# Branch B's query and key projections as four Strassen pairs in a stage of their own

## Chip, core and metric

One core of a Trainium2 chip runs the whole layer in one launch. The metric is device time in microseconds (us), the median of the runs. Of the core's engines, TensorE (PE, with PEld for its weight loads) does matmuls and transposes, VectorE (DVE), ScalarE (ACT) and GpSimd (POOL) work on tiles, and SyncE (SP) issues most DMAs.

## What is computed

An encoder layer is applied to two sequences, of 512 and of 1024 tokens, with 1024 features each; what concerns this change:

```
xn = RMSNorm(x);  z = xn @ W_in -> q_A k_A v_A q_B k_B v_B gate_A gate_B
branch A: grouped-query attention (8 query heads, 2 key heads, 64 wide, q/k normed, rotary)
branch B: 8 heads of neighbourhood attention: a key window of 8 rows x 16 columns on a
          grid 64 wide, learned relative bias; q_B, k_B are 512 columns each
mix = (sigmoid(gate_A) * (o_A @ W_pA) + sigmoid(gate_B) * (o_B @ W_pB)) @ W_out
x = x + mix;  x = x + relu(RMSNorm(x) @ W_up)^2 @ W_down;  final RMSNorm
```

All is float32. A matmul operand is split into a high part that the fp32r format holds and a remainder; `mm3` forms one product from three matmuls: high by high, high by low, low by high.

## The kernel before

`run` works through one sequence: the short one first (`NB == 1` block of 512 tokens), then the long one (`NB == 2`). The MLP follows for both. Within `run`, for each of the two key heads `g` of branch A, stage `phR` projects q, k, v (and v of branch B) and stage `phA` does the attention in units of one head and 512 queries, eight per `g` in the long sequence. Then stage `phB` does branch B, and `phG` the merge and `W_out`.

The gates need 128 x 8 x 3 large matmuls in all for the long sequence. They are generators (`gate`) put into `fill`: each `fill.pull(n)` traces n steps of them, a step being three matmuls of 128x128 by 128x512, so that TensorE has work while the softmax of the stage runs. In `phA`, each unit has eight key chunks (`kc`); in each, four transposes of P, the split of P by ScalarE and VectorE, two matmuls into o, and one pull in six of the eight chunks. What is left is drained at the end of the stage. In `phB`, a unit is a head and a strip of 16 columns (32 units); in each, `s_unit` (scores, bias, softmax), `t_unit` of the unit before (transposes) and `v_unit` of the one before that, with five or six pulls between.

Queries and keys of branch B are projected in `phB` by `qkproj`, one pair of heads at a time: for the first pair at the stage's start, for each of the next three within units 6 and 7 of the eight that precede it. A projection of 128 columns takes 8 feature slices x `mm3` for each of two token blocks, for q and for k: 96 matmuls a pair, 384 in all. From PSUM the result goes by ScalarE (high) and VectorE (low) straight to the tiles `qB` and `kB`. Each head's high and low parts lie in the two halves of the 128 partitions, so that one matmul sums over both.

The 8 KB-per-partition tiles (xn, q, k, v strips, gate weights) are slots of two pools: `s8r` with 11 slots on the right, `s8l` with 6 on the left. A new tile waits until a slot is free.

The order on each engine is made by a planner: it takes instructions whose inputs and buffers it expects to be ready, the earlier traced first. `tc.keep_in_program_order` pins an instruction behind the one traced before it on its engine.

The MLP's up projection (`up`) is already a Strassen scheme of seven products on 128x128 by 128x384 matmuls. Its operands are made by `up_steps` and, for the activations, by `pair_t`, in which some sums lie on GpSimd.

Of the kernel before, what the change touches and what calls it, by code (L numbers as in the profile page):

```python
# [61 lines left out]
def encoder(ctx: ExitStack, tc: tile.TileContext, xs, outs, w):  # L62
# [316 lines left out]
    def run(tr, nxt, first):  # L379
# [89 lines left out]
        def load_v(g, alloc, pin=False):  # L469
            return load_cols(win, 1792 + 256 * g, 256, f"v{N}_{g}", alloc, pin)  # L470

        early = {}
        for g in range(2):
            with phase(f"phR{N}_{g}") as ph:
                xn_of = {}
                fresh = g == 0 and tr.ready < NT
# [190 lines left out]
            with phase(f"phA{N}_{g}") as ph:  # L667
                units = [(h, qb) for h in range(4) for qb in range(NB)]
                PP = {}

                def s_tile(u, j):
                    h, qb = u
                    nm = f"{N}_{g}_{h}_{qb}_{j}"
                    q0 = (qb * 4 + j) * P
                    lhs = qT[h % 2][:, h // 2, q0 : q0 + P]
                    s = big(f"s{nm}")[:, :T]
                    for kb in range(NB):
                        ks = slice(kb * 512, kb * 512 + 512)
# [24 lines left out]

                for j in range(4):
                    s_tile(units[0], j)
                    fill.pull(2)
                queue = []
                LAG = 2
                for ui, u in enumerate(units):
                    h, qb = u  # L710
                    if first:
                        bias_row(g * 4 + ui)
                        if g == 0 and ui == 1:
                            early["a"] = load_a(1)
                        if g == 0 and ui == 2:
                            early["v"] = load_v(1, slot)
                    nxt_u = units[ui + 1] if ui + 1 < len(units) else None
                    sdone = 0
                    for kc in range(NT):
                        pt = mm(f"pT{N}_{g}_{h}_{qb}_{kc}")  # L720
                        for j in range(4):
                            nc.tensor.transpose(  # L722
                                pt[:, j * P : (j + 1) * P], PP[u, j][:, kc * P : (kc + 1) * P], ident
                            )
                        hi = ph.tile([P, 512], F32R, tag="pth", name=f"pth{N}_{g}_{h}_{qb}_{kc}", bufs=3)
                        lo = ph.tile([P, 512], F32R, tag="ptl", name=f"ptl{N}_{g}_{h}_{qb}_{kc}", bufs=3)
                        nc.scalar.activation(hi, pt, AF.Copy)  # L727
                        nc.vector.tensor_tensor(lo, pt, hi.bitcast(F32), op=ALU.subtract)  # L728
                        queue.append((u, kc, hi, lo))
                        if nxt_u is not None:  # L730
                            while sdone < 4 and kc >= ((0, 1, 3, 4) if NB == 2 else (0, 0, 1, 2))[sdone]:
                                s_tile(nxt_u, sdone)
                                sdone += 1

                        fill.pull(1 if NB == 1 or kc % 4 < 3 else 0)
                        if len(queue) > LAG:
                            pv(*queue.pop(0))
                fill.drain()
                for item in queue:
                    pv(*item)  # L740

        mA = {}
        wp_b = []
# [44 lines left out]
        with phase(f"phB{N}") as ph:  # L788
# [4 lines left out]
            def prep(h):  # L793
                rc = ph.tile([P, 16, 48], F32, tag="rect", name=f"rect{N}_{h}", bufs=2)
                nc.sync.dma_start(rc, biases[:, :, h].rearrange("r c i j -> (r c) i j"))
                rects[h] = rc
                v = slot([P, 4, rows // 4, P], F32R, f"vs{N}_{h}")
                for j in range(4):
                    c0 = (0, 8, 24, 32)[j]
                    for a in range(4):  # L800
                        nc.sync.dma_start(
                            v[a * 32 : a * 32 + 32, j, :, :].bitcast(F32),
                            vd[:, h, :].rearrange("(k a c) d -> a c k d", a=4, c=GRID_W)[a, c0 : c0 + 32],
                        )
                strips[h] = v

            def load_qk(pr):
                return (
                    load_cols(win, 768 + pr * P, P, f"bq{N}_{pr}"),
                    load_cols(win, 1280 + pr * P, P, f"bk{N}_{pr}"),  # L810
                )

            def qkproj(pr, wqk, dest):
# [4 lines left out]
                for tb in range(NB):  # L818
# [31 lines left out]
                    for e in range(2):  # L850
# [4 lines left out]
                        for os_ in (hs, ls):  # L855
                            nc.vector.tensor_tensor(
                                kT[e][os_, 1, cs], pk[hs], kT[e][hs, 0, cs].bitcast(F32), op=ALU.subtract
                            )

            qk = {}  # L860
            def s_unit(u):
                h, j = u
# [84 lines left out]
                    hi, lo = (oX3[0][ps, i, j * nq : (j + 1) * nq] for i in range(2))  # L947
                    finish_o(o, nq, None, ph, f"B{nm}", (hi, lo, ps))

            prep(0)  # L950
            fill.add(gate(3328, zg[1]))
            wqk = load_qk(0)
            fill.pull(1)
            for _ in qkproj(0, wqk, qk):
                pass
            units = [(h, j) for h in range(8) for j in (1, 2, 0, 3)]
            n = len(units)
            LS, LV = (1, 1) if NB == 2 else (2, 1)
# [1 line left out]
            for i in range(n + LS + LV):  # L960
                if i < n - 8:
                    f = (5 if i < LS else 2 + i % 2) if NB == 1 else 5 + (i % 3 > 0)
                else:
                    f = 3 + i % 2 if NB == 1 else 7
                if i < n:
                    s_unit(units[i])
                    if units[i][1] == 1 and units[i][0] + 1 < 8:
                        prep(units[i][0] + 1)
                    if i % 8 == 6 and i + 2 < n:

                        qp = qkproj(i // 8 + 1, wqk, qk)
                        for _ in range(NC8):
                            next(qp)
                    if i % 8 == 7 and qp is not None:
                        for _ in qp:
                            pass
                        qp = None
                        if i + 1 < n - 8:
                            wqk = load_qk(i // 8 + 2)
                fill.pull(f // 2)  # L980
                if 0 <= i - LS < n:
                    t_unit(units[i - LS])
                if i == n - (12 if first else 8):
                    pa = proj_a(ph)
                    next(pa)
                if i == n - 8:
                    fill.drain()
                    fill.add(pa)
                if i == 3:
                    wqk = load_qk(1)  # L990
                if qp is not None and NB == 2:
                    for _ in range(NC8):
                        next(qp)
                fill.pull(f - f // 2)
                if 0 <= i - LS - LV < n:
                    v_unit(units[i - LS - LV])
# [710 lines left out]
```

## Time and profile before

| | us |
|---|---|
| median of 3 runs | 2173.95 |
| lowest and highest run | 2173.1, 2175.7 |
| profiled execution, span from its first to its last instruction | 2172.2 |
| the last two stages before the merge: branch A of `g = 1`, and branch B, of the long sequence | 660 to 791, 791 to 1097 |

The profile names a group by line, engine, operation and tiles (out<-in). A busy time is the union of the instructions' times; a matmul's time includes its way through the array, so matmuls that follow each other overlap, and the distance of their starts is what each costs.

### The profile page before, as it was taken

The numbers are of one execution on the slowest core, as the hardware profiler recorded it, in microseconds if no ns is written. First come the engines' busy times: TensorE is split into PE (matmuls) and PEld (weight loads), VectorE is DVE, ScalarE is ACT, GpSimd is POOL, SyncE is SP. The second block draws the span as 40 slices with busy tenths as digits, with TensorE's granted clock in tenths as the row PEclk, the third lists the DMA queues.
The fourth block names the chain that finished last, engine by engine and source line by source line (L and its number), as shares of the span: only waits on it lengthen the run. The fifth ranks groups of instructions, "written<-read, shape, count | busy, mean of one in ns | idle before, by whom it ended". The sixth has DMA issues, their size and how long they took to land. (4 is left out here: it accounts for less than half of the span.)

```text
span 2172.2 us, 32392 instructions
## 1 busy us (share of the span) xinstructions
PE 2135.6 (98%) x11162; PEld 1867.9 (86%) x11162; DVE 1456.1 (67%) x2837; ACT 1109.3 (51%) x2379; POOL 349.4 (16%) x458
## 2 busy tenths in 40 slices
PE   8999999999999999999999999999999999999998
PEld 7788778888898888888888899998999988888886
DVE  6675566777756754555772777778777777769663
ACT  5654553556645744545531466656556643433452
POOL 2232210433233313322300200003000000000000
PEclk9999999999999999999999999999999999999999
DMA  5436457620122132423464656568544799788551
GB/s 166 144 104 179 137 145 249 211 71 28 45 75 86 44 92 88 125 80 110 136 195 137 202 180 195 179 226 223 158 156 155 234 347 343 224 268 290 175 194 68
DMA packets 319773, 350.94 MB, mean 162 GB/s; under 512 B 31352, under 2 KB 255224, under 8 KB 319609
## 3 DMA queue, kind: packets, MB, share of 16 engines
q1 hardware_dynamic: 277927, 279.65, 41.4%
q10 hardware_dynamic: 36002, 52.19, 6.9%
q0 software_dynamic: 5680, 17.04, 2.7%
q8 instruction: 88, 1.44, 0.3%
q14 instruction: 76, 0.62, 0.1%
HBM read 264.85 MB, written 87.88 MB: 162 GB/s over the span
## 5 line engine op out<-in xcount | busy, mean ns | idle before, releaser
L192 PE MATMUL dn<-wd,ah 128*128 128x512 f32 x624 | 243.0, 389 | 0.0
L193 PE MATMUL dn<-wd,al 128*128 128x512 f32 x624 | 243.0, 389 | 0.0
L191 PE MATMUL dn<-wd,ah 128*128 128x512 f32 x624 | 243.0, 389 | 0.0
L1184 ACT ACTIVATE ah<-ar 128x512 fp32r<-128x512 f32 x168 | 103.9, 627 | 195.1 <-PE dn L192 176.8
L1185 DVE TENSOR_TENSOR al<-ar,ah 128x512 fp32r<-128x512 f32 x168 | 115.1, 693 | 73.9 <-ACT ah L1184 66.7
L192 PEld LDWEIGHTS dn<-wd,ah 128*128 128x128 f32 x624 | 117.2, 188 | 24.4
L193 PEld LDWEIGHTS dn<-wd,al 128*128 128x128 f32 x624 | 117.2, 188 | 24.2
L191 PEld LDWEIGHTS dn<-wd,ah 128*128 128x128 f32 x624 | 117.2, 188 | 24.1
L728 DVE TENSOR_TENSOR ptls<-pTs,pths 128x512 fp32r<-128x512 f32 x160 | 107.7, 686 | 37.9 <-ACT pths L727 37.0
L727 ACT ACTIVATE pths<-pTs 128x512 fp32r<-128x512 f32 x160 | 94.1, 597 | 74.0 <-PE pTs L722 71.8
L688 POOL TENSOR_SCALAR ps<-ps,rls 128x1024 f32<-128x1024 f32 (+1 forms) x96 | 96.6, 1007 | 216.2 <-DVE rls L687 197.2
L682 DVE TENSOR_REDUCE nms<-ss 128x1 f32<-128x1024 f32 (+1 forms) x96 | 99.9, 1041 | 25.4 <-PE ss L680 25.0
L191 PE MATMUL gpss<-xs_0h,w_gs 128*128 128x512 f32 x256 | 106.2, 415 | 0.8 <-DVE rlbs L898 0.7
L685 ACT ACTIVATE ps<-ss,nms 128x1024 f32<-128x1024 f32 (+1 forms) x96 | 93.2, 972 | 22.4 <-DVE nms L682 20.0
L722 PEld LDWEIGHTS pTs<-ident,ps 128*128 128x128 f32 x640 | 78.2, 140 | 28.1 <-POOL ps L688 4.2
L193 PE MATMUL gpss<-xs_0h,w_gs 128*128 128x512 f32 x256 | 101.7, 397 | 0.0
L192 PE MATMUL gpss<-xs_0l,w_gs 128*128 128x512 f32 x256 | 101.6, 397 | 0.0
L722 PE MATMUL pTs<-ident,ps 128*128 128x128 f32 x640 | 98.9, 274 | 1.3 <-DVE ptls L728 0.6
L176 POOL TENSOR_TENSOR rs_f<-ms_f,mhalf 128x1 f32<-128x1 f32 x6 | 4.0, 667 | 590.7 <-DVE ms_f L172 590.7
L1184 ACT ACTIVATE A<-S 128x512 fp32r<-128x512 f32 x128 | 75.9, 623 | 29.4 <-DVE S L1247 22.1
L891 DVE CUSTOM_DVE_ANT_0 sbss<-sbs,bms 128x384 f32<-128x384 f32 (+1 forms) x96 | 48.6, 508 | 58.2 <-issue 34.1
L191 PE MATMUL ud<-B,A 128*128 128x384 f32 x256 | 85.8, 335 | 1.4 <-DVE c L1302 1.4
(325 smaller groups left out, 6444.8 us busy)
## 6 DMA issues: line engine op xcount, KB each, us to landing
ar<-ud SPq DMA_DIRECT2D x120, 512.0 KB
br<-in_w_mlp_down_dram SPq DMA_DIRECT2D x72, 512.0 KB
rawu<-in_w_mlp_up_dram SPq DMA_DIRECT2D x64, 512.0 KB
ud<-c ACTq DMA_DIRECT2D x128, 192.0 KB
raw_gs<-in_w_in_dram SPq DMA_DIRECT2D x32, 512.0 KB
zgs<-sgs ACTq DMA_DIRECT2D x48, 256.0 KB
ud<-cs SPq DMA_DIRECT2D x64, 192.0 KB
raw_os<-in_w_out_dram SPq DMA_DIRECT2D x16, 512.0 KB
```

The lines of the kernel that those rows point to most:

```text
L191: nc.tensor.matmul(out, ah, bh, start=start, stop=False, **kw)
L192: nc.tensor.matmul(out, ah, bl, start=False, stop=False, **kw)
L193: nc.tensor.matmul(out, al, bh, start=False, stop=stop, **kw)
L682: nc.vector.tensor_reduce(nm_, s, axis=AX.X, op=ALU.max, negate=True)
L685: nc.scalar.activation(p, s, AF.Exp, bias=nm_, accum_out=l)
L688: nc.gpsimd.tensor_scalar(p, p, rl, 1.0, op0=ALU.mult, op1=ALU.mult)
L722: nc.tensor.transpose(pt[:, j * P : (j + 1) * P], PP[u, j][:, kc * P : (kc + 1) * P], ident)
L727: nc.scalar.activation(hi, pt, AF.Copy)
L728: nc.vector.tensor_tensor(lo, pt, hi.bitcast(F32), op=ALU.subtract)
L891: nc.vector.tensor_tensor_reduce(out=sb, in0=so, in1=bm, op0=ALU.add, op1=ALU.min, scale=-1.0, scalar=3e38, accum_out=nm_)
L1184: nc.scalar.activation(hi, src, AF.Copy)
L1185: nc.vector.tensor_tensor(lo, src, hi.bitcast(F32), op=ALU.subtract)
```

## The change

For the long sequence only, a new stage `wide` (`phS`) stands between `phA` of `g = 1` and `phB`. It computes q and k of branch B in four sets of 256 columns (q and k of heads 0 to 3, then of 4 to 7). Each set is a 2x2 block product in Strassen's form: 512 features x 512 features, 128 columns x 128 columns, 512 tokens x 512 tokens, with seven products of four slices x `mm3` where eight would be usual. `form` makes the seven weight operands, `put` forms the four results, splits them and stores them to DRAM (`qd`, `kd`) from ScalarE's queue. Of the seven forms of x, three (0, 5 and 4) are xn's own blocks; the other four (2, 1, 3, 6) are made by `x_forms` in 16 chunks on GpSimd, VectorE and ScalarE, into eight slots of `s8r`: four chunks in units 2 to 5 of `phA`, four in unit 7, eight in `wide`.

In `phA` of `g = 1` a unit pulls five gate steps instead of six, and the stage's end no longer drains them: `wide` does so after its first weight forms. In `phB`, `qkproj` is gone; `ask_q` and `ask_k` load the tiles of a pair from DRAM by SP, two DMAs of 512 KB each for q and for each head's k, in unit 3 (q and the first k) and unit 7 (the second k) of the eight before. At the stage's start one gate step and then eight are pulled. The short sequence keeps its way.

```
+        def x_forms():
+            (h1, l1), (h2, l2) = tr.xhl[0], tr.xhl[1]
+            XF[0], XF[5], XF[4], XF[7] = (h1[0], l1[0]), (h1[1], l1[1]), (h2[1], l2[1]), (h2[0], l2[0])
+            pin = tc.keep_in_program_order
+            def chunk(i, a, b, c):
...
+                pin(nc.gpsimd.tensor_tensor(lo, al, bl, op=ALU.subtract))
+                pin(nc.vector.tensor_tensor(d, ah, bh, op=ALU.subtract))
+                pin(nc.gpsimd.tensor_tensor(d, d, lo.bitcast(F32), op=ALU.add))
+                def rest():
+                    pin(nc.scalar.activation(hi, d, AF.Copy))
+                    pin(nc.vector.tensor_tensor(lo, d, hi.bitcast(F32), op=ALU.subtract))
...
+        def wide(ph):
+            def kf(shape, dt, name):
+                return ph.tile(shape, dt, tag="kf", name=name, bufs=9)
...
+            def form(n, i):
...
+                if i == 1:
+                    nc.vector.tensor_tensor(S[0], a21, a22, op=ALU.add)
+                    nc.vector.tensor_tensor(S[1], S[0], a11, op=ALU.subtract)
+                if i == 3:
+                    nc.vector.tensor_tensor(a21, a11, a21, op=ALU.subtract)
+                if i == 4:
+                    nc.vector.tensor_tensor(S[1], a12, S[1], op=ALU.subtract)
+                src = {0: a11, 1: S[1], 2: S[0], 3: a21, 4: S[1], 5: a12, 6: a22}[i]
+                t = kf([P, 2, 4, P], F32R, f"sa{N}_{n}_{i}")
+                nc.scalar.activation(t[:, 0], src, AF.Copy)
+                nc.vector.tensor_tensor(t[:, 1], src, t[:, 0].bitcast(F32), op=ALU.subtract)
...
+            def first_two(n):
...
+                prod(n, a, 0, False)
+                nc.scalar.activation(s1, a, AF.Copy)
+                prod(n, a, 5, True)
+                put(n, 0, 0, a)
+            def others(n, side):
...
+                prod(n, bk, 1, False)
+                step()
+                nc.vector.tensor_tensor(s1, bk, s1, op=ALU.add)
...
+                prod(n, c, 2, False)
+                step()
+                nc.scalar.activation(s5, c, AF.Copy)
+                nc.vector.tensor_tensor(s5, s5, s1, op=ALU.add)
+                prod(n, c, 4, True)
+                step()
+                put(n, 0, 1, c, s1)
+                prod(n, d, 3, False)
+                step()
+                put(n, 1, 1, d, s5, s5)
+                prod(n, d, 6, True)
+                step()
+                put(n, 1, 0, d, s1, s1)
...
+            for n in range(2):
+                for i in (0, 5):
+                    form(n, i)
+                    x_form_step()
+            form(0, 1)
+            fill.drain()
+            first_two(0)
+            x_form_step()
+            form(0, 2)
+            x_form_step()
+            first_two(1)
+            form(0, 4)
+            x_form_step()
+            form(0, 3)
+            x_form_step()
+            form(0, 6)
...
@@ phA
-                        fill.pull(1 if NB == 1 or kc % 4 < 3 else 0)
+                            fill.pull(1 if kc in (0, 2, 3, 5, 6) else 0)
+                            if ui in (2, 3, 4, 5):
+                                if kc == 6:
+                                    x_form_step()
+                            elif ui == 7 and kc % 2 == 1:
+                                x_form_step()
...
@@ phB
+            def ask_k(pr, e):
+                kT = slot([P, 2, T], F32R, f"kB{N}_{pr}_{e}")
+                qk[pr][1].append(kT)
+                for i in range(2):
+                    nc.sync.dma_start(kT[64 * i : 64 * i + 64, :, :].bitcast(F32), kd[pr][64 * e : 64 * e + 64, :, :])
...
-            wqk = load_qk(0)
-            fill.pull(1)
-            for _ in qkproj(0, wqk, qk):
-                pass
+                ask_q(0)
+                ask_k(0, 0)
+                prep(0)
+                fill.pull(1)
+                ask_k(0, 1)
+                fill.pull(8)
```

More of the change, by code (lines that the diff above doesn't have):

```diff
@@ L470, in load_v @@
             return load_cols(win, 1792 + 256 * g, 256, f"v{N}_{g}", alloc, pin)
+        XF, x_todo, x_rest = {}, [], []
+        x_room = [lambda name: rawp.tile([P, 512], F32, tag="raw", name=name)]
+        def x_forms():
[3 more added lines that the diff above has]
+            def chunk(i, a, b, c):
+                if i not in XF:
+                    XF[i] = tuple(slot([P, 4, 512], F32R, f"xf{n_}{N}_{i}") for n_ in "hl")
+                hi, lo = (t[:, c, :] for t in XF[i])
+                (ah, al), (bh, bl) = ([t[:, c, :].bitcast(F32) for t in XF[n]] for n in (a, b))
+                d = x_room[-1](f"xd{N}_{i}_{c}")
+                pin(nc.gpsimd.tensor_tensor(lo, al, bl, op=ALU.subtract))
[4 more added lines that the diff above has]
+                    pin(nc.vector.tensor_tensor(lo, d, hi.bitcast(F32), op=ALU.subtract))
+                x_rest.append(rest)
+            for i, a, b in ((2, 7, 0), (1, 4, 2), (3, 4, 7), (6, 5, 1)):
+                x_todo.extend(partial(chunk, i, a, b, c) for c in range(4))
@@ L472, in run @@
         early = {}
         for g in range(2):
+            if g == 1 and NB == 2:
+                x_forms()
             with phase(f"phR{N}_{g}") as ph:
@@ L733, in run @@
                                 sdone += 1
-                        fill.pull(1 if NB == 1 or kc % 4 < 3 else 0)
+                        if NB == 1 or g == 0:
+                            fill.pull(1 if NB == 1 or kc % 4 < 3 else 0)
+                        else:
+                            fill.pull(1 if kc in (0, 2, 3, 5, 6) else 0)
[3 more added lines that the diff above has]
+                            elif ui == 7 and kc % 2 == 1:
+                                x_form_step()
+                            if ui in (3, 4, 5, 6) and kc == 1:
+                                x_form_end()
                         if len(queue) > LAG:
                             pv(*queue.pop(0))
-                fill.drain()
+                if NB == 1 or g == 0:
+                    fill.drain()
                 for item in queue:
                     pv(*item)
+        if NB == 2:
+            with phase(f"phS{N}") as ph:
+                wide(ph)
         mA = {}
@@ L858, in qkproj, with ask_q @@
                             )
+            def ask_q(pr):
+                qT = slot([P, 2, T], F32R, f"qB{N}_{pr}")
+                qk[pr] = (qT, [])
+                for i in range(2):
+                    nc.sync.dma_start(
+                        qT[64 * i : 64 * i + 64, :, :].bitcast(F32),
+                        qd[pr][:, i, :].rearrange("(e d) t -> d e t", e=2),
+                    )
+            def ask_k(pr, e):
+                kT = slot([P, 2, T], F32R, f"kB{N}_{pr}_{e}")
+                qk[pr][1].append(kT)
+                for i in range(2):
+                    nc.sync.dma_start(kT[64 * i : 64 * i + 64, :, :].bitcast(F32), kd[pr][64 * e : 64 * e + 64, :, :])
             qk = {}
@@ L948, in v_unit @@
                     finish_o(o, nq, None, ph, f"B{nm}", (hi, lo, ps))
-            prep(0)
+            if NB == 1:
+                prep(0)
             fill.add(gate(3328, zg[1]))
-            wqk = load_qk(0)
-            fill.pull(1)
-            for _ in qkproj(0, wqk, qk):
-                pass
+            if NB == 1:
+                wqk = load_qk(0)
+                fill.pull(1)
+                for _ in qkproj(0, wqk, qk):
+                    pass
+            else:
+                ask_q(0)
+                ask_k(0, 0)
+                prep(0)
+                fill.pull(1)
+                ask_k(0, 1)
+                fill.pull(8)
             units = [(h, j) for h in range(8) for j in (1, 2, 0, 3)]
@@ L968, in run @@
                         prep(units[i][0] + 1)
-                    if i % 8 == 6 and i + 2 < n:
+                    if NB == 2:
+                        if i % 8 == 3 and i < n - 8:
+                            ask_q(i // 8 + 1)
+                            ask_k(i // 8 + 1, 0)
+                        if i % 8 == 7 and i < n - 8:
+                            ask_k(i // 8 + 1, 1)
+                    elif i % 8 == 6 and i + 2 < n:
                         qp = qkproj(i // 8 + 1, wqk, qk)
@@ L988, in run @@
                     fill.add(pa)
-                if i == 3:
+                if i == 3 and NB == 1:
                     wqk = load_qk(1)
-                if qp is not None and NB == 2:
-                    for _ in range(NC8):
-                        next(qp)
                 fill.pull(f - f // 2)
```

106 lines of the change are left out of this document (added).

## The prediction, made before the changed kernel ran

> **What bounds the kernel now.** I read the head of the page first, then busy time by stage, then who ended TensorE's waits.
>
> ```profile
> span 2172.2 us, 32392 instructions
> ...
> PE 2135.6 (98%) x11162; PEld 1867.9 (86%) x11162; DVE 1456.1 (67%) x2837; ACT 1109.3 (51%) x2379; POOL 349.4 (16%) x458
> ```
>
> ```profile
> core 0: us, PE busy (x) PEld busy (x) DVE busy (x) ACT busy (x) POOL busy (x), PEclk, DMA share, GB/s
> 660.00:793.00 133.00, 132.91 (x709) 108.50 (x708) 93.71 (x148) 85.79 (x151) 37.27 (x33) 1.00 0.19 57
> 793.00:1097.00 304.00, 299.80 (x1543) 250.37 (x1542) 171.41 (x468) 149.31 (x328) 83.36 (x112) 1.00 0.37 111
> ```
>
> The two stretches are branch A of the long sequence's second key head (660 to 793) and its branch B (793 to 1097). TensorE is busy in all of the first and all but 4.2 us of the second, at the full clock. The list of TensorE's waits has only small entries; the two that lie in branch B are
>
> ```profile
> PE gpss L191 <- ACT sgs L412: 1.5, 1, 1.5
> ...
> PE sbs L888 <- DVE kBs L856: 1.3, 2, 0.8
> ```
>
> So TensorE's instruction stream is the bound. A product that is left out is worth its whole slot, and any wait that is put in costs its whole length, unless the planner finds other TensorE work for it. VectorE has 39 us to spare in the first stretch and 133 in the second: slack that is spread out, which matters below.
>
> **Step 1, products left out.** The projections of q and k in branch B are these groups (first and last of twelve alike, in branch B of the long sequence), and this is their pace:
>
> ```profile
> L191 PE MATMUL pkbs<-xs_0h,w_bks 128*128 128x512 f32 x32 | 12.7, 398 | 0.0
> ...
> L192 PE MATMUL pkbs<-xs_1l,w_bks 128*128 128x512 f32 x32 | 12.5, 389 | 0.0
> ```
>
> ```profile
> 791.40 0.39 PE L191 MATMUL pqbs<-xs_0h,w_bqs 128*128 128x512 f32 x1
> ...
> 793.89 0.39 PE L193 MATMUL pqbs<-xs_0h,w_bqs 128*128 128x512 f32 x1
> ```
>
> Twelve groups of 32 are 384 matmuls. The 389 ns is the latency of a pipelined one; from the first row to the last are eleven starts, 2.49/11 = 0.226 us each, and that is the slot. The change runs 4 sets x 7 products x 4 slices x 3 = 336 of the same shape: 48 fewer, 48 x 0.226 = **10.9 us** less. By the loops this cannot fail to happen. One product is 12 x 0.226 = 2.72 us.
>
> **Step 2, fewer gate steps in branch A.** A gate step (3 x 0.226 = 0.68 us) is pulled 5 times in a unit instead of 6. Before, 15 ahead of the units and 48 in them are 63 of the 65 steps; after, 15 + 40 = 55. Ten steps, 6.8 us, run at the start of the new stage. Their sum doesn't change; they become cover there.
>
> **Step 3, the sums and differences of x.** Sixteen chunks (four forms, four column slices), each two GpSimd tensor_tensors and two VectorE ones of 128x512, all with both inputs in SBUF, and one ScalarE copy. Eight chunks lie in branch A (one in each of units 2 to 5, four in the last), eight in the first part of the new stage. The same operations on the same shapes occur in the hand-over to the MLP:
>
> ```profile
> L327 POOL TENSOR_TENSOR B<-ta,B x12: 1277/1294/1622, 1211.9 to 1500.1; 128x512 fp32r<-128x512 f32 x12
> ```
>
> ```profile
> L327 DVE TENSOR_TENSOR B<-ta,B 128x512 fp32r<-128x512 f32 x6 | 7.1, 1183 | 0.0
> L327 DVE TENSOR_TENSOR B<-pt,B 128x512 fp32r<-128x512 f32 x9 | 5.9, 683 | 0.6 <-ACT B L324 0.6
> ```
>
> ```profile
> 1218.77 0.68 DVE L338 TENSOR_TENSOR ta<-pt,y 128x512 f32<-128x512 f32 x1
> ...
> 1220.64 1.29 DVE L327 TENSOR_TENSOR B<-pt,B 128x512 fp32r<-128x512 f32 x2
> 1221.84 1.67 DVE L327 TENSOR_TENSOR B<-ta,B 128x512 fp32r<-128x512 f32 x1
> ```
>
> ```profile
> 1218.81 1.29 POOL L327 TENSOR_TENSOR B<-ta,B 128x512 fp32r<-128x512 f32 x1 [2.06 <-ACT B L324]
> 1221.69 1.28 POOL L327 TENSOR_TENSOR B<-ta,B 128x512 fp32r<-128x512 f32 x1 [1.59 <-ACT B L324]
> ```
>
> A GpSimd operation takes 1.29 us. VectorE runs two in 1.29, so a following one adds 0.60. At 1218.77 VectorE's operation reads PSUM and SBUF and runs beside GpSimd's at 0.68. At 1221.84 it reads SBUF twice: GpSimd's ends at 1222.97, VectorE's at 1223.51, 0.54 after. It waited for the whole rest of GpSimd's operation, and the mean of this kind is 1183 ns against 683. I read this as exclusion: one of the two at a time.
>
> Now the sum. Up to the sixth product of the first set (the one that needs the last form of x), the new stage must put through: GpSimd 8 chunks x 2 = 16 x 1.29 = 20.6 us; VectorE's doubly-SBUF operations 8 differences + 9 remainders of x, and 9 remainders and 4 sums of the weights' forms = 30 x 0.60 = 18.0 us. One after the other: 38.6 us. TensorE has until then ten gate steps 6.8, the first two products of two sets 10.9, and four products of the first set 10.9 = 28.6 us. Missing: **10 us**. If a meeting cost only the mean stretch (1183 less 683, 0.50 us), VectorE would need 18.0 + 16 x 0.50 = 26 us, less than TensorE's 28.6, and the term would be 0; the row at 1221.84 speaks for the first reading. The Trainium skill (SBUF — State Buffer, "SBUF: two separate sides") calls the shared port pair "an exclusive lock, not a bandwidth split", held for the whole instruction; by it the term is the 10 too. Bounds: each chunk is a chain (GpSimd and VectorE, GpSimd, ScalarE, VectorE) that need not pack, and four chunks in branch A's last unit are already 4 x (2.58 + 1.20) = 15 us of this resource against some 11 us of TensorE there, so 19 at the top; at the bottom 3, if products of the second set, which need only earlier forms, are put in the gap. I take 10, since these second products wait for weight forms that queue on the same VectorE behind the x steps. In branch A itself the lag costs 0 to 2 us, 0.7 taken: the remainder of P there reads PSUM, and gate steps can fill.
>
> **Step 4, the rest of the stage.** VectorE's work there is about 28 + 16 operations for the weights, 20 sums and 8 remainders and 32 short ones on outputs, 17 on x: 89 x 0.60 + 32 x 0.22 = 60 us (0.22: four in 0.88, row below), in 83 us of TensorE work (336 x 0.226 + 6.8). Past the start it keeps up. But product 5 accumulates on the bank that ScalarE copies after product 0, 4 on that of product 2, and 6 on the one that VectorE has to read first:
>
> ```profile
> L1184 ACT ACTIVATE A<-S 128x512 fp32r<-128x512 f32 x128 | 75.9, 623 | 29.4 <-DVE S L1247 22.1 <-PE ua L193 5.4 <-DVE S L1249 1.9
> 797.66 0.88 DVE L838 SCALAR_TENSOR_TENSOR qBs<-pqbs,qBs 64x128 fp32r<-64x128 f32 x4 [4.67 <-ACT qBs L836]
> ```
>
> ```profile
> 791.31 0.33 ACTq L413 DMA_DIRECT2D zgs<-sgs  x1
> ```
>
> About 0.9 us for a copy with its signals, twelve places; most can be filled with another product, the last set's cannot all. 1 to 5 us, **2** taken. The 24 stores are issued on ScalarE's queue at 0.33 us each, 8 us in 83; it has room.
>
> **Step 5, the clock.**
>
> ```profile
> 411.30:413.40 2.10, 0.36 (x4) 0.16 (x2) 1.61 (x9) 1.47 (x11) 0.78 (x2) 1.00 0.77 221
> 413.70:417.10 3.40, 3.31 (x12) 2.80 (x11) 2.20 (x8) 1.48 (x7) 2.73 (x5) 0.50 0.40 131
> ...
> 954.50:957.00 2.50, 1.04 (x6) 0.57 (x4) 2.44 (x5) 2.30 (x5) 0.00 (x0) 1.00 0.00 0
> ```
>
> After TensorE stood for 1.74 of 2.1 us, the granted clock was 0.50 for 3.4 us: 1.7 us lost. After the gap at 955 it was not. Stalls of 2 us and more in step 3 can each cost that: 0 to 5, one, **1.7**, taken. The Trainium skill (TensorE: Matmul & The Clock Gate, "Part 1: The HAM clock gate") drops the clock only after an idle window of about 3.4 us; by that rule this term would be 0 where the waits stay shorter. The row at 411 differs from it.
>
> **Step 6, branch B without projections.** It loses 384 matmuls and, with them, 20 to 25 us of cover at its start (four times 24 matmuls, 21.7 us) that hid the mask's load:
>
> ```profile
> 789.35 0.64 POOL L790 DMA_DIRECT2D msks<-in_mask_dram  x1 [11.88 <-issue]
> 797.61 3.54 POOL L874 TENSOR_TENSOR bms<-rects,msks 128x384 f32<-128x384 f32 x4 [7.62 <-DMA msks<-in_mask_dram]
> ```
>
> Mask 8.3 us after its issue, then 0.9 for the first bias, then softmax: some 12 us before the first transposes. In place are 8 gate steps (5.4 us), two units' matmuls and the gate steps between (about 6). Cost 0 to 6, **2** taken. q and k come back by 512 KB loads on SP's queue, asked four to five units ahead:
>
> ```profile
> 884.80:891.30 6.50, 6.50 (x38) 5.50 (x37) 3.19 (x10) 3.27 (x8) 1.17 (x2) 1.00 0.46 137
> L899 POOL TENSOR_SCALAR pbs<-pbs,rlbs 128x384 f32<-128x384 f32 x64 | 38.5, 608 | 105.1 <-DVE rlbs L898 93.3 <-PE ptbs L911 11.7
> ```
>
> A unit with gate fill takes 6.5 us, so that is 25 us and more ahead; 12 MB at the 137 GB/s already seen there would be 88 us spread over some 217 (304 less 87 of projections): hidden. A later load waits only for a slot of 11, which the finished pair frees. The unit holds six gate steps (4.1 us), so 2.4 us of its own. Gate steps last to unit 20 (1 + 8 pulled ahead, 17 in three units), so units 21 to 23 have none, where before the last projections stood: each then lasts as long as its softmax chain or GpSimd's two 0.6 and two 0.9 us operations, about 3.1. 3 x 0.7 = **2** (0 to 4; attention A's projection can fill). Gone are the waits above, 1.5 + 0.8: **-2.3**.
>
> **Sum.** -10.9 + 0.7 + 10 + 2 + 1.7 + 2 + 2 - 2.3 = +5.2 us on the span of 2172.2, so 2177.4; the median of the runs, 2173.95, stands 1.75 above the span, so **2179 us**.
>
> **Rivals.**
> - *The planner fills the gap (faster).* Step 3 costs 3, the clock nothing, branch B's start 0: -10.9 + 0.7 + 3 + 2 + 2 - 2.3 = -5.5, **2168**. For it: branch B's waits are small although its order is as tangled, so the planner does move ready TensorE work forward. Against: the second set's forms lie on the contended VectorE. It decides when TensorE's wait in the stage's first 45 us is under 5 us.
> - *Cancelled.* The exclusion costs 5 to 6 us: **2174**.
> - *Branch B starts late (slower still).* Mask, rows of bias and the first k wait for buffers that the new stage holds to its end, and 8 us of its start lie bare: **2187**. For it: the 8.3 us of the mask. Against: the planner can ask it once the first buffers are free, before the last set ends.
> - *Exclusion in full.* Step 3 at 19 us: 2188, by the chain's bound.
>
> **How the numbers follow.** Forecast 0.42 (2175 to 2184), filled 0.26, cancelled 0.12, late start 0.1, full exclusion 0.1. 0.2% is 4.3 us, about what a measurement here can tell from no change. Filled gives nearly all of faster, 0.25; cancelled and the forecast's lower edge (a quarter of it) give same, 0.22; the rest is slower, 0.53. Range 2166 to 2190: below, the filled case less its own doubt of 2; above, the two slower cases.
>
> **What would show it.** 336 matmuls where 384 were, at 0.226 us a start. In the new stage's first 45 us: VectorE's x and weight remainders at a mean of 1 us and more, GpSimd busy nearly throughout, and 8 to 14 us in which TensorE stands, its waits ended by VectorE's remainders of x or of the weights. Past that, TensorE over 95% busy. Units 21 to 23 of branch B at some 3 us each. Wrong, if TensorE is over 90% busy in those 45 us, if VectorE's remainders there stay at 0.69, or if the time is lost in branch B's first 20 us instead.

## The result and the profile after

The changed kernel takes 2230.05 us, median of four runs (2228.2 to 2232.0), against 2174.26 us before: 1.025 times as long, interval 1.0235 to 1.0264. The forecast was 2179, its range 2166 to 2190; the loss is some eleven times the one forecast. The head of the page:

```profile
span 2228.6 us, 32450 instructions
...
PE 2145.9 (96%) x11114; PEld 1865.5 (84%) x11114; DVE 1500.2 (67%) x2861; ACT 1114.7 (50%) x2391; POOL 397.6 (18%) x490
```

48 matmuls fewer, and the time in which TensorE isn't busy went from 37 to 83 us. Busy time by stretch, with the columns of the prediction's table, first of the kernel before:

```profile
672.00:793.00 121.00, 120.91 (x656) 99.05 (x655) 86.68 (x137) 80.30 (x140) 35.02 (x31) 1.00 0.14 42
793.00:903.00 110.00, 108.90 (x543) 90.14 (x542) 57.08 (x158) 52.34 (x111) 30.67 (x42) 1.00 0.38 109
903.00:1050.00 147.00, 144.15 (x752) 120.81 (x751) 82.62 (x231) 74.76 (x165) 42.85 (x58) 1.00 0.37 110
1050.00:1150.00 100.00, 99.75 (x483) 82.76 (x482) 77.00 (x159) 42.94 (x81) 10.45 (x14) 1.00 0.57 180
```

and of the changed kernel, where the second row is the new stage and the last two are branch B:

```profile
672.00:793.00 121.00, 119.21 (x643) 96.19 (x642) 97.12 (x148) 83.03 (x146) 59.09 (x48) 1.00 0.09 27
793.00:903.00 110.00, 92.89 (x362) 71.01 (x361) 79.77 (x123) 36.51 (x63) 24.50 (x16) 0.92 0.49 144
903.00:1050.00 147.00, 135.74 (x708) 113.07 (x707) 64.73 (x196) 67.21 (x163) 55.88 (x77) 0.94 0.68 182
1050.00:1150.00 100.00, 83.56 (x433) 68.09 (x432) 61.28 (x160) 45.86 (x107) 28.00 (x37) 0.90 0.52 162
```

TensorE stands 46.6 us in these rows, 4.3 before: 17.1 in the stage, 11.3 and 16.4 in branch B. And its clock falls, which in these rows it didn't before. Over 96 rows of 5 us each, from 670 to 1150, busy time times one less the granted clock adds to 17.6 us. So 42.3 more of standing + 17.6 of clock - 10.9 of products = 49.0, of the 56.4 by which the span grew. Of the other 7.4, 3.8 are standing outside these rows (82.7 less 46.6, against 36.6 less 4.3 before). The last 3.6 weren't located. They may lie in time that counts as busy: a matmul after a wait counts its whole 0.39 us and more, where a pipelined one costs 0.226.

The largest waits of TensorE, now in three places:

```profile
PE ppas L191 <- ACT oXs L180: 12.5, 2, 10.6
PE sbs L1127 <- DVE nmbs L1130: 12.4, 8, 7.5
PE w0s L193 <- DVE sas L563: 4.4, 1, 4.4
```

**The start of the stage.** VectorE and GpSimd, by time:

```profile
797.69 0.68 DVE L493 TENSOR_TENSOR xfls<-xds,xfhs 128x512 fp32r<-128x512 f32 x1
798.29 1.78 DVE L554 TENSOR_TENSOR S0s<-rawss,rawss 128x512 f32<-128x512 f32 x1
800.00 1.75 DVE L563 TENSOR_TENSOR sas<-rawss,sas 128x512 fp32r<-128x512 f32 x1
```

```profile
797.94 1.59 POOL L489 TENSOR_TENSOR xds<-xds,xfls 128x512 f32<-128x512 f32 x1 [4.85 <-DVE xds L488]
799.48 1.72 POOL L487 TENSOR_TENSOR xfls<-xs_1l,xs_1l 128x512 fp32r<-128x512 f32 x1
```

The two engines take turns. GpSimd's operation at 797.94 ends at 799.53, and VectorE's sum, begun at 798.29, ends 0.54 us after that; GpSimd's next ends at 801.20, and VectorE's next 0.55 us after it. So each VectorE operation waits out GpSimd's: 1.78 and 1.75 us for work of 0.68. TensorE's 4.4 us wait is for such a weight remainder.

**The start of branch B.** The last store of the stage, then the mask, the first bias sums and the score matmul that waited for the VectorE step behind them:

```profile
902.90 0.52 ACTq L580 DMA_DIRECT2D kds<-hls  x1
```

```profile
908.45 0.64 POOL L1014 DMA_DIRECT2D msks<-in_mask_dram  x1 [74.72 <-DMA rects<-biases]
...
917.23 3.52 POOL L1113 TENSOR_TENSOR bms<-rects,msks 128x384 f32<-128x384 f32 x4 [8.13 <-DMA msks<-in_mask_dram]
...
918.78 1.01 PE L1127 MATMUL sbs<-kBs,qBs 128*128 128x384 f32 x2 [7.53 <-DVE nmbs L1130]
```

GpSimd was idle for 74.7 us before it asked for the mask. I read this as memory: the mask's tile lies where the stage's tiles lay, and these were held until their stores had landed. The bias rows are named as the last releaser here; in a run below, where the same wait ends at 907.6, the store `kds<-hls` is.

**The end of branch B.** The last gate matmul starts at 1053.60. Then SyncE's queue, ScalarE and TensorE:

```profile
1066.26 8.18 SPq L1025 DMA_DIRECT2D vss<-vds  x16
...
1074.49 0.43 SPq L216 DMA_DIRECT2D raw_pas<-in_w_proj_a_dram  x1
...
1077.67 0.63 ACT L180 ACTIVATE w_pas<-raw_pas 128x512 fp32r<-128x512 f32 x1 [10.05 <-DMA raw_pas<-in_w_proj_a_dram]
...
1080.03 0.80 PE L191 MATMUL ppas<-oXs,w_pas 128*128 128x512 f32 x1 [10.62 <-ACT oXs L180]
```

Attention A's projection is the only filling left after the gates, and its weights are asked behind the sixteen loads of the last head's v. From 1071.0 to 1077.7 no compute engine works.

### The profile page after: what moved, and what is told of

It is laid out like the page before. It is cut to its first block, busy times and chain, and to the rows that moved or that the text cites. A ratio compares the mean times of both kernels' runs of the same rounds, so it can differ in the third digit from the quotient of the medians.

```text
span 2228.6 us, 32450 instructions
## 1 busy us (share of the span) xinstructions
PE 2145.9 (96%) x11114; PEld 1865.5 (84%) x11114; DVE 1500.2 (67%) x2861; ACT 1114.7 (50%) x2391; POOL 397.6 (18%) x490
## 3 DMA queue, kind: packets, MB, share of 16 engines
q1 hardware_dynamic: 276263, 292.23, 42.3%
## 5 line engine op out<-in xcount | busy, mean ns | idle before, releaser
L191 PEld LDWEIGHTS dn<-wd,ah 128*128 128x128 f32 x624 | 117.1, 188 | 24.5
L937 DVE TENSOR_TENSOR ptls<-pTs,pths 128x512 fp32r<-128x512 f32 x160 | 107.4, 684 | 32.8 <-ACT pths L936 32.3
L891 DVE TENSOR_REDUCE nms<-ss 128x1 f32<-128x1024 f32 (+1 forms) x96 | 99.8, 1040 | 23.8 <-PE ss L889 22.8
L1436 DVE TENSOR_TENSOR A<-S,A 128x512 fp32r<-128x512 f32 x128 | 84.5, 686 | 4.2 <-ACT A L1435 4.1
```

What stands on the lines that cost most here:

```text
L191: nc.tensor.matmul(out, ah, bh, start=start, stop=False, **kw)
L1436: nc.vector.tensor_tensor(lo, src, hi.bitcast(F32), op=ALU.subtract)
```

## The experiments

Theory at the start: three separate losses (exclusion in the stage, a late mask, an end without filling), all from the stage's place and the forms of x. The kernel before, measured beside them, took 2174.7 to 2176.0 us.

**Forms of x on VectorE alone, in the stage.** In `chunk` (`x_room` has a second entry once the stage has begun):

```
+ eng = nc.vector if len(x_room) > 1 else nc.gpsimd
- pin(nc.gpsimd.tensor_tensor(lo, al, bl, op=ALU.subtract))
+ pin(eng.tensor_tensor(lo, al, bl, op=ALU.subtract))
...
- pin(nc.gpsimd.tensor_tensor(d, d, lo.bitcast(F32), op=ALU.add))
+ pin(eng.tensor_tensor(d, d, lo.bitcast(F32), op=ALU.add))
```

> Only the eight chunks of x forms that lie in the new stage change: their two GpSimd operations run on VectorE. In the changed kernel VectorE is 100% busy from 800 to 830, its SBUF-SBUF operations take 1.76 us where one of GpSimd's lies beside them and 0.68 alone, and TensorE stands or runs at a low clock for some 24 us in the stage. Theory (exclusion: GpSimd's 1.6 us shut VectorE out): a chunk then costs VectorE 4 x 0.68 = 2.7 us instead of 2 x 1.6 + 2 x 0.68 = 4.5; eight chunks save 14 us of VectorE's time, TensorE's wait falls by 9 to 14 us, the kernel takes 2216 to 2222. Rival (VectorE is simply overloaded, GpSimd only helps): 16 more operations of 0.68 us, 11 us, make it 2235 to 2242.

Measured: 2218.22 us, 11.8 less than the changed kernel. The total is the theory's, the place only in part. VectorE's operations are at 0.68 us again, but the 16 added ones keep it full (19.1 and 20.0 us busy of 800 to 820 and 820 to 840). From branch A's first transposes to the stage's last product are 223.3 us instead of 227.6. A larger part, 8.6 us, came between the last product and the last gate step (144.6 us instead of 153.2). The mask was asked at 888.2 there instead of 908.4, though nothing was changed in that place. That this is the cause isn't shown: the two runs that follow ask mask rows earlier still and leave the same stretch at 150.0 and 152.1 us.

**The early mask rows.** A tile of 2 x 384 mask values gets its own memory and is loaded in the stage; the column tile S has two buffers instead of three; the other four rows are loaded where the mask was.

```
+ early_msk.append(mp.tile([P, 2, 384], BF16, tag="mska", name=f"mska{N}", bufs=1))
...
+ for i in range(2):
+     nc.gpsimd.dma_start(early_msk[0][:, i], w["mask2"][:, 3 * i + 1])
```

> The mask rows that branch B's first two units need are asked in the middle of the new stage into memory of their own (2 x 0.75 KB a partition, one column tile S less); the other four rows are asked where the mask was. Theory: the 7.5 us in which TensorE waits before 918.8 and the lower clock after it (2.7 us) come from the mask, which waits for the last store of k (landed at 907.6) because its tile lies where the stage's tiles lay: 8 to 10 us go, 2220 to 2223. Rival: the bias and softmax tiles lie there as well and wait for the same stores, then only the 8.1 us of the load count less some other wait: 2 to 5 us, 2225 to 2228. Second rival: GpSimd's DMA issue in the stage delays something else, no gain.

Measured: 2231.27 us, no gain, which is the second rival's number. The four later loads stood in GpSimd's queue until 907.9 and the first bias sum behind them. So it was done once more with these loads traced behind the first unit's sums:

> As the run with the early mask rows, but the four later mask loads, which wait for the stage's memory, are traced behind the first unit's bias sums, so that GpSimd isn't held by them. Theory (start of branch B: mask behind the last store): the first bias sum starts by 909 instead of 917, TensorE's 7.5 us before 918.8 shrink to under 2, and 5 to 9 us go: 2221 to 2225. Rival (the next wait, for the second k at 907.6 plus its landing or for v of head 1, ends as late): 2227 to 2231.

Measured: 2230.56 us, again nothing; the rival was right. The first sum moved from 917.2 to 912.5 only, and now waited for the bias rows, a load of SyncE's queue that was issued at 907.1:

```profile
907.08 0.34 SPq L1038 DMA_DIRECT2D rects<-biases  x1
...
907.61 2.16 POOL L1236 DMA_DIRECT2D msks<-in_mask_dram  x4 [74.90 <-DMA kds<-hls]
...
912.47 1.77 POOL L1132 TENSOR_TENSOR bms<-rects,mskas 128x384 f32<-128x384 f32 x2 [2.70 <-DMA rects<-biases]
```

The load of the rows had itself waited, 3.0 us, for a store `kds<-hls`. So the mask was not the only thing of branch B that waits for the stage's stores. The stage itself stood 3 us longer in this run (20.9 against 17.7 us between branch A's last transposes and the last product), perhaps from the missing buffer of S; that wasn't separated.

**Attention A's projection three units earlier.** `proj_a` is traced at unit 21 instead of 24, ahead of the last head's v:

```
- if i == n - (12 if first else 8):
+ if i == n - (12 if first else 11):
      pa = proj_a(ph)
      next(pa)
+     if not first:
+         fill.add(pa)
- if i == n - 8:
+ if i == n - 8 and first:
...
```

> Attention A's projection is put into the filling at unit 21 instead of 24, so its loads are queued on SyncE ahead of the sixteen loads of the last head's v, and its steps follow the last gate step at once. Theory: the stall of 10.6 us at 1069 to 1080, the waits of units 21 to 24 before it (3.4 us), 1.9 us at 1085 and the clock of 0.50 after it (4.7 us) come from these loads standing behind v's: 14 to 20 us go, 2210 to 2216. Rival: the loads wait for the slots that xn holds until the last gate step (1054), whatever their place: they come at 1058 and only 8 to 12 go, 2218 to 2222. Second rival: with four slots more taken the last pair's k or v comes late, no gain.

Measured: 2223.21 us, 6.8 less, just above the first rival's bounds. The projection begins at 1064.1 instead of 1080.0, but then the last head's v is late (issued 1079.5 to 1091.7, before 1066.3 to 1074.4) and the scores wait. I read this as too few slots for both; no run with more slots tests it.

**Ordinary products in the same stage.** Sixteen results of eight slices each, from xn's own blocks, no `x_forms`, no sums; for each set `n`:

```
...
+ for f in range(2):
+     for half, xi in enumerate(((0, 5), (7, 4))):
+         a = mm(f"w{N}_{n}_{f}{half}")
+         for kb in range(2):
+             part(n, a, ops[n][2 * f + kb], xi[kb], kb == 1)
+         put(n, f, half, a)
```

> The stage stays, through DRAM, at its place, but forms q and k as eight ordinary block products: 384 matmuls, no forms of x at all, no sums of weights or results. Theory (what the change costs is mostly its place, not the product scheme): products +10.9 us, the stage's 24 us of stalls gone, branch B's start and end stay at their 10 and 27: 2230 - 24 + 11 = 2213 to 2221, still 40 above the kernel before. Rival (the x forms spoil all that follows, in branch A too): 2185 or less.

Measured: 2184.64 us, 9.4 above the kernel before (1.0038, interval 1.0026 to 1.005). Here my theory fell, and the rival's bound of 2185 held. Place and DRAM cost 9 us, not 40. The same code of branch B in which TensorE stands 27.7 us behind the seven-product stage stands 9.9 behind this one: 7.4 in the last two rows, and 2.5 in the first, since branch B begins here at 878:

```profile
793.00:903.00 110.00, 107.51 (x485) 88.74 (x484) 31.75 (x83) 27.91 (x53) 11.21 (x15) 1.00 0.75 214
903.00:1050.00 147.00, 140.28 (x769) 117.65 (x768) 80.65 (x247) 81.07 (x193) 64.30 (x86) 0.98 0.64 177
1050.00:1150.00 100.00, 99.35 (x487) 82.42 (x486) 74.49 (x156) 42.60 (x86) 9.93 (x12) 1.00 0.55 175
```

So something in the forms of x reaches into branch B. A new theory: their eight slots, held to the stage's end. Behind ordinary products v of head 0 is asked at 829 and of head 1 at 852; in the changed kernel at 889 and 909.

**The slots alone.** Ordinary products again, while eight tiles that nothing computes with hold the slots as long as the forms of x would:

```
+ HT[i] = [slot([P, 4, 512], F32R, f"xf{n_}{N}_{i}") for n_ in "hl"]
+ for t in HT[i]:
+     nc.gpsimd.memset(t[:, 0, 0:1].bitcast(F32), 0.0)
```

> The kernel with the stage of eight ordinary products (2184.6), and beside it eight slots of s8r are held, by tiles that nothing computes with, from where the forms of x would be made to the fourth set's products, as in the changed kernel. Theory (slots): with eight of eleven slots held, branch B's first two v tiles and its second k cannot be asked until the stage is over (changed kernel: 889 to 934 for v of heads 0 and 1; ordinary products: 829 to 862), the loads stay just in time for the whole of branch B, and the 25 us by which the changed kernel's branch B is longer (last product to the merge, 249 against 224) come from this: 2200 to 2212. Rival (the slots are not the limit; the lost time in branch B comes from the plan that follows the x forms): within 4 us of 2184.6.

Measured: 2197.91 us, 13.3 more. The stage is as long as without the hold; the loss lies mostly where the gate steps end:

```profile
903.00:1050.00 147.00, 134.27 (x734) 111.70 (x734) 73.20 (x229) 76.64 (x185) 61.39 (x84) 0.95 0.71 195
```

A little less than expected, and above the rival. In all of branch B TensorE stands 17.2 us instead of 9.9 (27.7 in the changed kernel): the slots are some two fifths of that difference. The weights of attention A's projection show how it comes about: first asked at 973.1 behind the ordinary products (950.4 in the kernel before), they are asked at 1039.8 with the slots held, behind the last gate step, as in the changed kernel (1074.5).

**Seven products without forms of x, and the same with the slots held.**

```
...
+ XF[2], XF[1], XF[3], XF[6] = XF[7], XF[0], XF[4], XF[5]
  def chunk(i, a, b, c):
+     return
```

> The seven-product stage with everything of it but the forms of x: no sums or differences of x, the four forms are replaced by plain blocks of xn (so q and k of branch B aren't those of the reference), and the eight slots stay free. Theory (the x forms cost the stage some 25 to 30 us through VectorE and, through their slots, branch B some 25): 2230 - 50 to 2230 - 60, that is 2170 to 2180: the product saving of 10.9 against about ten for the place. Rival (the weights' forms and the sums of results are as dear as those of x): above 2190.

> As the run without forms of x, but the eight slots are held as in the changed kernel by tiles that nothing computes with; q and k of branch B aren't those of the reference. Theory (two prices, work of x and slots): the stage is as short as without the forms, branch B as long as in the changed kernel: 15 to 27 us more than without the hold, 2190 to 2205. Rival (slots cost nothing): as without the hold, within 4 us.

Measured: 2184.76 us, and 2195.14 with the hold, 10.4 more. The slots' price is confirmed a second time, though below the expected 15; here the same weights are asked at 1041.2 instead of 977.5. The first number surprised, and neither theory nor rival had it: with the forms of x for nothing, seven products take as long as eight.

**Without GpSimd's operations.** All 16 chunks keep VectorE's and ScalarE's operations, the slots and the order:

```
- pin(nc.gpsimd.tensor_tensor(lo, al, bl, op=ALU.subtract))
  pin(nc.vector.tensor_tensor(d, ah, bh, op=ALU.subtract))
- pin(nc.gpsimd.tensor_tensor(d, d, lo.bitcast(F32), op=ALU.add))
```

> All 16 chunks of x forms without their two GpSimd operations (the remainders' difference is left out, so q and k of branch B lose their low part's share); VectorE's and ScalarE's operations, the slots and the order stay. Theory (exclusion): VectorE's SBUF-SBUF operations in the stage fall from 1.2 and 1.6 us to 0.69, the stage loses 8 us of stalls and 3 to 7 of low clock: last product at 880 to 886 instead of 900.7, and the whole 2205 to 2216. Rival (VectorE's own number of operations): VectorE stays 95% busy from 800 to 840 and the stage keeps 18 us or more of stalls and low clock, 2222 or more.

Measured: 2213.56 us, 16.5 less, with the last product at 885.4, inside the theory's bounds. The weights' remainders between 796 and 840, first in the changed kernel, then here:

```profile
L563 DVE TENSOR_TENSOR sas<-rawss,sas 128x512 fp32r<-128x512 f32 x6 | 9.5, 1576 | 5.2 <-ACT sas L562 5.2
```

```profile
L561 DVE TENSOR_TENSOR sas<-rawss,sas 128x512 fp32r<-128x512 f32 x9 | 6.2, 684 | 2.8 <-ACT sas L560 2.8
```

1576 ns against 684, and nine of them done where six were. That is the exclusion, shown by taking the other engine away. Its price alone is not shown: without these operations each chunk's chain is shorter too. From branch A's last transposes to the stage's last product this run takes 100.2 us, the changed kernel 114.6, and the run with the stage's operations moved to VectorE 110.3.

**Five gate steps in every unit of branch B**, where 5, 6, 6 stood:

```
- f = (5 if i < LS else 2 + i % 2) if NB == 1 else 5 + (i % 3 > 0)
+ f = (5 if i < LS else 2 + i % 2) if NB == 1 else 5
```

> Branch B pulls five gate steps in every unit up to 23 instead of six on average (5 or 6). Theory (units 20 to 23 without filling cost 3.4 us of waits, then 10.6 us until attention A's loads are in): the last gate step moves to unit 22, the units under filling become shorter by 0.45 us each, the bare units fall from four to two; TensorE stands 2 to 5 us less: 2224 to 2228. Rival (xn's slots, and so the loads of attention A, are let go only after the last gate step, so each us that the steps last longer comes back at the end): 2229 to 2233.

Measured: 2222.22 us, 7.8 less, more than expected. The last gate step ends 8.4 us later (1062.4), the first projection starts 2.8 us earlier (1077.2): the bare stretch falls from 26.0 to 14.8 us.

**Mended branch B under both kinds of products.** Early mask rows and five gate steps, with ordinary products, and with seven products without forms of x:

> The stage of eight ordinary products with the early mask rows and five gate steps in every unit. It stood 2.5 us before the first bias and 9.5 us (7.2 of waits, 2.3 of low clock) at the end of the gate steps. Theory (place costs only these two): 2174 to 2181, no better than the kernel before, since it has the same 384 products and still one bare stretch. Rival (they are independent of both edits): 2184.

> The seven-product stage without the forms of x (plain blocks of xn in their place, q and k of branch B aren't the reference's), with the early mask rows and five gate steps: what the products alone could bring with branch B mended. Theory (the weights' forms, the sums of the results and their waits for banks take back what the 48 products give): within 4 us of the ordinary products with the same edits, 2172 to 2180. Rival (they only looked dear because branch B's end hid the gain): 2164 to 2170.

Measured: 2176.28 us (1.0005 of before, interval 0.9995 to 1.0015) and 2176.73 us (1.0006, 0.9994 to 1.0017). Both lie in the theory's bounds. With both edits the place costs nothing that can be measured (the bare stretch behind the last gate step is 1.7 us here, 11.7 without them), and the seven products still bring nothing. The seven-product stage and the ordinary one:

```profile
793.00:903.00 110.00, 103.24 (x443) 81.59 (x442) 62.61 (x132) 39.79 (x73) 12.65 (x18) 0.98 0.75 211
```

```profile
793.00:903.00 110.00, 108.21 (x492) 89.42 (x491) 32.80 (x88) 28.60 (x55) 14.05 (x20) 1.00 0.76 211
```

VectorE's work doubles (32.8 to 62.6 us) and TensorE stands 6.8 us instead of 1.8, 3.3 of it among the products, where the ordinary ones don't stand at all. From branch A's first transposes to the end of branch B the two take 421.6 and 423.0 us: 1.4 of the 10.9 is left, and the medians show not even that. (They are counted from there because the profiled execution of the first was already 5.7 us later at that point, ahead of all edits; why, stays open.)

**The two edits that gained, on the real kernel.**

> The two edits to the changed kernel that gained, together: the stage's eight chunks on VectorE alone, and five gate steps in every unit. Theory (the losses lie in different stages and add): 2230 - 12 - 8 = 2207 to 2213, so the seven-product kernel stays 33 or more above the kernel before. Rival (both gains came from the same late part of branch B): 2215 to 2219.

Measured: 2210.74 us, 19.3 less; the parts add up (11.8 + 7.8). It is still 35 us above the kernel before. No version was faster than the kernel before.

## Why the prediction was wrong, step by step

The time lies above the range because three terms were too small or missing: the work of forming x (step 3), what the seven-product stage costs besides (step 4), and the slots that the forms hold (step 6); each also lowered the clock (step 5). The prices, each a difference of two kernels: ordinary products in their place +9.4 (2184.64 against 2175.26); seven instead of eight, forms of x for nothing, +0.1; their slots +10.4 (2195.14 against 2184.76); the work of forming them +34.9 (2230.05 against 2195.14), of which GpSimd's operations are 16.5. Together +54.8; measured +55.8. The median of the kernel before moved by 1.3 us between the sets of runs, so the +0.1 can't be told from nothing.

- **Step 1, products left out: right.** 336 matmuls, with a median distance of 0.227 us in the stage. They are worth their slot only where the stream keeps flowing; here it didn't.
- **Step 2, gate steps moved:** nothing speaks against it; the gate steps end at unit 20 (1054, when its transposes begin), where step 6 had put them.
- **Step 3, forms of x: mechanism right, size too small.** I took 10 us, at most 19. From branch A's last transposes to the stage's last product the changed kernel takes 114.6 us, and 90.8 without the forms and with the slots held: 23.8 us, 13.6 of them standing (17.7 against 4.1) and 7.4 low clock. Over the whole kernel the work of the forms costs 34.9. The term used 1.29 us for a GpSimd operation; in turn with VectorE it takes 1.59 and 1.72. And it counted TensorE's first products as cover, though these waited for weight remainders in the same queue. Of its own signs for the first 45 us (793 to 838) two came: 11.6 us of standing, and VectorE's remainders of x and of the weights at a mean of 1.01 us. Two did not: GpSimd was busy for 24.5 us, not nearly throughout, and past that, from 845 to 903, TensorE was busy for 52.5 of 58 us, 91% and not over 95%.
- **Step 4, the rest of the stage: too small.** 2 taken, 5 at most. Without forms of x the stage should have been 10.9 us shorter than the ordinary one. From branch A's last transposes to the last product it takes 96.0 against 95.2 us, 90.8 against 95.2 with the slots held, and 92.5 against 95.2 in the mended pair: 6.5 to 11.7 us are lost. In the mended run 2.0 and 1.1 us are waits for copies of first results (ScalarE's s5), as the step had it; the rest lies in time that counts as busy and stays open.
- **Step 5, the clock:** 1.7 taken, 5 at most; 17.6 measured. I counted one stall. There were six stretches of low clock: three in the stage, one at branch B's start, one at 1016 and one at its end.
- **Step 6, branch B:** 4 us in two terms, 10 at most; it stands 27.7 us, 3.1 before in the same rows. Missing was a term for the slots, which cost 13.3 and 10.4 us in two pairs of runs. The prediction counted eleven and let a later load wait "only for a slot of 11, which the finished pair frees", but not that the forms hold eight of them until the stage ends, so that the loads behind it come late. And units 21 to 23 were short, as forecast (3 us each), but what came after them was late: attention A's loads stand behind v's. Spreading the gate steps alone gave back 7.8 us, which the 2 us for these units couldn't have held.

The rival "branch B starts late" named one of the places, at 8 us of 56: from 10 to 30 us behind the last product TensorE stands 7.9 us and loses some 2.6 to the clock. None of the rivals had the sum of all three, and each loss was priced as if the others left the clock at 1.

## What to carry to other kernels

A product that is left out of a saturated TensorE stream is worth its slot only if what makes its operands has a place to run; count the work of the slowest helper engine in the stage that bounds it, with operations of VectorE and GpSimd that have two inputs in SBUF in series, and compare it with the TensorE work that is left. Count buffers as well as time: a stage that holds the slots of the next one's loads makes these late long after it has ended. And try the new stage first with the ordinary computation in it and the new operands for nothing: those two runs, at 2185 each, said that there was nothing to win.

## What the runs showed of the hardware

The clock, in rows of 2 us around a short stall of the changed kernel:

```profile
1012.00:1014.00 2.00, 1.76 (x11) 1.31 (x9) 0.89 (x4) 1.94 (x5) 1.98 (x3) 1.00 1.19 315
1014.00:1016.00 2.00, 0.63 (x2) 0.30 (x2) 1.18 (x4) 0.83 (x3) 0.06 (x1) 1.00 0.98 355
1016.00:1018.00 2.00, 1.65 (x4) 1.10 (x4) 0.96 (x7) 1.66 (x3) 1.59 (x3) 0.55 0.36 129
1018.00:1020.00 2.00, 1.48 (x4) 1.38 (x5) 2.00 (x4) 0.00 (x0) 1.74 (x2) 0.50 1.06 229
1020.00:1022.00 2.00, 2.00 (x7) 1.71 (x7) 0.40 (x1) 0.00 (x0) 0.00 (x0) 0.50 0.92 188
1022.00:1024.00 2.00, 2.00 (x10) 1.71 (x10) 0.11 (x1) 0.38 (x1) 0.00 (x0) 0.74 0.81 145
```

TensorE stood 1.6 us in the first two rows, no wait above 1.1 us, and the clock was about a half for the next 7 us: in the last four rows busy time times one less the clock gives 3.0 us, on top of the waits. The Trainium skill (TensorE: Matmul & The Clock Gate, "Part 1: The HAM clock gate") has the clock fall after an idle window of about 3.4 us; these rows don't agree with it as a limit on a single wait.

VectorE's 0.68 us and GpSimd's 1.29 us operation, both with two inputs in SBUF, became 1.75 and 1.6 to 1.7 us when they met in turns. The Trainium skill (SBUF — State Buffer, "SBUF: two separate sides") says that one of the two blocks in full; the trace agrees, and the run without GpSimd's operations shows it.
